# Seven block products for a convolution's input projections, and a modulation stream moved into the layer before it

## The chip, the cores and the metric

The kernel runs on one core of a Trainium2 chip, in one launch. The metric is the device time of one execution in microseconds, here the median of three runs. The times below come from these runs and from one execution recorded by the hardware profiler.

## The reference, cut to what matters

Two blocks follow each other. The change touches the second, which has two layers. Each layer has a mixer and a feed-forward part; shift, scale and gate of both come from a vector `c` (the modulation).

```python
for i in range(2):
    mods = silu(c) @ w_ada[i] + b_ada[i]          # 1024 -> 6 x 1024
    sh1, sc1, g1, sh2, sc2, g2 = split(mods, 6)
    h = rms_norm(x, norm1_g[i]) * (1 + sc1) + sh1
    mix = s5_mixer(h) if i == 0 else short_conv_mixer(h)
    x = x + g1 * mix
    h = rms_norm(x, norm2_g[i]) * (1 + sc2) + sh2
    x = x + g2 * swiglu(h)                        # hidden width 2816
return rms_norm(x, final_g)

def short_conv_mixer(h):
    bg, cg, v = split(h @ w_in, 3)                # 1024 -> 3 x 1024
    return (bg * causal_conv3(cg * v)) @ w_out
```

There are 1024 tokens of width 1024, all in float32.

## The kernel before, in words

Activations lie transposed: 128 channels on the partitions, tokens along the free axis, in two halves of 512. A float32 product is made of three matmuls in a reduced-width form: each operand is split into a high part (ScalarE, line 105) and a low part (VectorE, line 113), and `mm3` (lines 119 to 121) adds high x high, high x low and low x high. A weight block is 128 x 512 (four 128 x 128 tiles).

Feed-forward layers (`phase_ffn`) go through groups of hidden blocks: first the input products of the group's blocks, then the output products with all of the group, which are added to x in memory by accumulating transfers from the POOL queue (line 2058), or, in the last group, to x on the chip. The input products of one hidden block, two row blocks (gate and up) by 1024 tokens by 1024 channels, are a `Unit`: a 2 x 2 by 2 x 2 block product in seven half-size products instead of eight, each of 12 matmuls. Its weight sums (S1 to S4) are made on VectorE from four loaded blocks, its token sums (T1 to T4) once per layer by `Quad.make`. The results are put together on VectorE (line 1940). `ffn_head` runs the first three hidden blocks while the norm of the second token half still comes in: the first block by eight ordinary products, the next two by seven each, in an order that uses the early tokens first.

`Weights` is the feed-forward layers' stream: a list of entries (load, make). `take` hands out the next split block after `fill` has issued loads until six entries are under way (`near` and `ready` together) and made splits until four are ready. Raw blocks have six buffers, split pairs six, sums two. The loads are issued by SyncE in order. A stream is set up at a layer's start and ends with it.

The convolution (`phase_conv`) does not use it. `Normed` writes the normed tokens in two parts. For each of eight blocks and each token half, three ordinary gemms of 24 matmuls give cg, v and bg (tiles pc, pv, pb); VectorE and ScalarE form cg * v, the three taps and the product with bg. Loads and splits come from `e.wload`, emitted when the phase starts. Then x is copied on the chip, and the output products (tile pco) follow.

The modulation is computed by `ada` as a background generator: columns of `w_ada` are loaded (SyncE, line 1316), multiplied by silu(c) and added up on VectorE (lines 1322 and 1324), summed over the partitions by a matmul with ones (tile pada), copied by ScalarE and stored as a row in memory by SyncE (line 1338). `e.tick()` advances it. The first layer's feed-forward half and two of the second layer's six parts run in the mixer's output stage, in tiles of 1024 columns; the other four run in the convolution, in tiles of 512 columns with two buffers.

The order of instructions on each engine comes from the order of the calls and a scheduler that puts ready work of other engines in between; an engine runs its own instructions in that order.

Of the kernel before, what the change touches and what calls it, by code (L numbers as in the profile page):

```python
# [14 lines left out]
P = 128  # L15
# [21 lines left out]
class Env:  # L37


    def __init__(self, ctx, tc, d, out):  # L40
# [15 lines left out]
        self.ident_r = c.tile([P, P], F32R, name="ident_r")  # L56
# [190 lines left out]
def phase_projections(e):  # L247
# [152 lines left out]
    bif = np_.tile([36, 1], F32, name="bif")  # L400
# [385 lines left out]
def phase_attention(e, r1, x, done):  # L786
# [41 lines left out]
    nlam = np_.tile([P, 1], F32, name="nlam")  # L828
# [468 lines left out]
def ada(e, tiles, L, mods, step, wait, ahead, s0=0, s1=6, w=T):  # L1297
# [3 lines left out]
    if s0 == 0:  # L1301
        cact = e.const.tile([P, 8], F32, name=f"ada{L}c")
        e.tc.keep_in_program_order(nc.scalar.activation(cact, e.col("c"), AF.Silu))
        mods[L] = e.const.tile([P, 48], F32, name=f"ada{L}"), cact
# [34 lines left out]
    rr = e.t2("adrr")[0:n, 0:P]  # L1339
    nc.sync.dma_start(out=rr, in_=row)  # L1340
    bb = e.t2("adb")[0:n, 0:P]
    nc.sync.dma_start(out=bb, in_=d["b_ada"][L][8 * s0:8 * s1])
# [309 lines left out]
def phase_mixer(e, mods, x, n, fg, nxt):  # L1652
# [61 lines left out]
    e.bg += [ada(e, wada, 0, mods, 4, 2, 4, 3), ada(e, wada, 1, mods, 4, 2, 4, 0, 2)]  # L1714
# [106 lines left out]
class Weights:  # L1821
# [15 lines left out]
    def block(self, src, more=False):  # L1837
# [3 lines left out]
        def load():  # L1841
# [7 lines left out]
            self.more.tile([P, 4, P], F32R, tag=t, name=t, bufs=4) for t in ("wh", "wl")])  # L1849
# [40 lines left out]
    def fill(self, ahead):  # L1890
# [3 lines left out]
        while self.near and len(self.ready) <= ahead:  # L1894
            self.ready.append(self.near.pop(0)[1]())
# [59 lines left out]
class Normed(Next):  # L1955


    def __init__(self, e, mod, i, x, name):
        super().__init__(e, name, self.pairs)
        self.x = x  # L1960
        self.mod, self.i = mod, i
        self.hT = [{} for _ in range(NB)]

    def pairs(self, h, r):
        nc, i = self.e.nc, self.i
        R = self.e.spread(r, self.e.np_, self.name)
        for b in range(NB):
            if b and b % 2 == 0:
                yield
            t = self.e.t2("hx")  # L1970
            A = self.mod[:, 8 + 24 * i + b:9 + 24 * i + b]
            B = self.mod[:, 24 * i + b:24 * i + b + 1]
            nc.vector.scalar_tensor_tensor(out=t, in0=self.x[b][h], scalar=A, in1=R,
                                           op0=ALU.mult, op1=ALU.mult)
            hi, lo = self.hT[b][h] = pair(self.e, b, h, self.name)
            nc.scalar.activation(hi, t, AF.Identity, bias=B)
            nc.vector.scalar_tensor_tensor(out=lo, in0=t, scalar=B, in1=hi.bitcast(F32),
                                           op0=ALU.add, op1=ALU.subtract)


def phase_ffn(e, L, mod, inp, nxt, xp, last):

    nc, d, q = e.nc, e.d, inp.q
    W = Weights(e, 6, 6, 2, 3, 6)
    e.ap = e.tc.alloc_tile_pool(name="ap", bufs=1, reuse_waits="tile")
    src = lambda f: [d["w_ffn_in"][L, f + NF * i] for i in range(2)]
    a = {}

    def use(f):

        s = {}

        def take(n, t):
            h = int(n[1])
            s[h, int(n[0])] = t
            if n[0] == "0":
                nc.scalar.activation(t, t, AF.Silu)
            if (h, 0) in s and (h, 1) in s:
                nc.vector.tensor_tensor(out=s[h, 1], in0=s[h, 1], in1=s[h, 0], op=ALU.mult)
                if f not in a:  # L2000
                    a[f] = tuple(xp.tile([P, T], F32R, tag="x", name=f"a{p}", bufs=NB) for p in range(2))
# [3 lines left out]
    def plan():  # L2005
        for f0, f1 in FGROUPS:
            for f in range(max(f0, 3), f1):
                W.add(*W.unit(src(f), [Unit.left[p] for p in Unit.order]))
            if f1 - f0 == 4:
                W.add(*(W.block(d["w_ffn_out"][L, m, :, f0:f1], f1 == NF and m >= 4) for m in range(NB)))  # L2010
            else:
                W.add(*(W.block(d["w_ffn_out"][L, m:m + 2, :, f0:f1].rearrange("m p f c -> p m f c"))
                        for m in range(0, NB, 2)))

    for gi, (f0, f1) in enumerate(FGROUPS):
        end = gi == len(FGROUPS) - 1
        fs = list(range(f0, f1))
        if gi == 0:
            ffn_head(e, W, inp, src, use, plan)
            fs = fs[3:]  # L2020
        for f in fs:
            e.tick()
            Unit(e, W, q, use(f)).run(Unit.order)
        parts = nxt.parts if end else Next.parts
        if end:
            pool = last()
            W.more = e.tc.alloc_tile_pool(name="wt", bufs=1, side="right", reuse_waits="tile")
            for m in range(NB):
                t = pool.tile([P, T], F32, tag="x", name=f"x{m}", bufs=NB)
                e.x[m] = [t[:, half(h)] for h in range(2)]  # L2030
            for h in range(2):
                for m in range(NB):
                    nc.scalar.dma_start(out=e.x[m][h], in_=inp.xd[m][:, half(h)])
        wo = {}
        for m, i in (order(NB, NB - 1, len(parts)) if end else
                     [(m, h) for m in (0, 1) for h in (1,)] + [(m, 0) for m in (0, 1)]
# [374 lines left out]
```

## Time and profile before

| what | us |
|---|---|
| median of three runs (2900.1 to 2903.42) | 2900.79 |
| the profiled execution | 2904.91 |
| its span, first to last instruction | 2903.1 |
| first feed-forward layer, from its first product | 1182.5 to 1854.4 |
| convolution, input products | 1854.45 to 2128.8 |
| convolution, output products | 2128.8 to 2218.1 |
| second feed-forward layer, from its first product | 2220.6 on |

PE is TensorE, DVE is VectorE, ACT is ScalarE, SP is SyncE. Busy time of PE is modelled at the matmuls' ends, which overlap, so the spacing of two starts says more than a duration. A wait is given as the engine's idle time and what ended it.

### The profile page before, as it was taken

The numbers are of one execution on the slowest core, as the hardware profiler recorded it, in microseconds if no ns is written. First come the engines' busy times: TensorE is split into PE (matmuls) and PEld (weight loads), VectorE is DVE, ScalarE is ACT, GpSimd is POOL, SyncE is SP. The second block draws the span as 40 slices with busy tenths as digits, with TensorE's granted clock in tenths as the row PEclk, the third lists the DMA queues.
The fourth block names the chain that finished last, engine by engine and source line by source line (L and its number), as shares of the span: only waits on it lengthen the run. The fifth ranks groups of instructions, "written<-read, shape, count | busy, mean of one in ns | idle before, by whom it ended". The sixth has DMA issues, their size and how long they took to land.

```text
span 2903.1 us, 38535 instructions
## 1 busy us (share of the span) xinstructions
PE 2849.6 (98%) x14112; PEld 2327.7 (80%) x14112; DVE 1825.2 (63%) x3585; ACT 1218.3 (42%) x2251; POOL 207.1 (7%) x270
## 2 busy tenths in 40 slices
PE   8999999999999999999999999999999999999998
PEld 7888788877778777788888888788887888888887
DVE  7988556388967964866455446765246754645465
ACT  6244553366746621633333343422234433333343
POOL 0000000000001000010101120000010011010110
PEclk9999999999999999999999999999999999999999
DMA  6465227553234653152534553354132345253543
GB/s 220 158 224 185 93 75 245 178 177 110 84 95 169 224 178 126 49 103 72 105 82 86 101 103 92 108 171 139 47 131 70 78 86 100 70 103 86 96 94 124
DMA packets 174709, 351.00 MB, mean 121 GB/s; under 512 B 19124, under 2 KB 38900, under 8 KB 173496
## 3 DMA queue, kind: packets, MB, share of 16 engines
q1 hardware_dynamic: 139448, 281.42, 30.0%
q0 software_dynamic: 26880, 54.54, 11.7%
q10 hardware_dynamic: 8192, 12.59, 1.3%
q8 instruction: 111, 1.82, 0.3%
q14 instruction: 78, 0.64, 0.1%
HBM read 246.71 MB, written 97.57 MB: 119 GB/s over the span
## 4 chain that ended last, share of the span: by engine, by line
PE 75%; issue 6%; DVE 5%; ACT 1%; DMA 1%; POOL 0%; ACTq 0%; DVEq 0%; POOLq 0%; SPq 0%
PE pu L119 9%; PE pu L121 9%; PE pu L120 9%; PE po L120 5%; PE po L119 5%; PE po L121 5%; PE pout L119 1%; PE pout L120 1%; PE pout L121 1%; PE pS L871 1%; PE pc L121 1%; PE pc L119 1%; PE pc L120 1%; PE pco L119 1%; PE pco L120 1%
## 5 line engine op out<-in xcount | busy, mean ns | idle before, releaser
L113 DVE TENSOR_TENSOR wl<-raw,wh 128x512 fp32r<-128x512 f32 x292 | 199.8, 686 | 245.3 <-ACT wh L105 239.5
L105 ACT ACTIVATE wh<-raw 128x512 fp32r<-128x512 f32 x292 | 182.5, 629 | 345.9 <-PE pu L120 191.3
L121 PE MATMUL po<-a,wl 128*128 128x512 f32 (+1 forms) x736 | 279.5, 380 | 1.2 <-DVE wl L113 1.2
L119 PE MATMUL po<-a,wh 128*128 128x512 f32 (+1 forms) x736 | 279.7, 381 | 0.2 <-ACT wh L105 0.2
L120 PE MATMUL po<-a,wh 128*128 128x512 f32 (+1 forms) x736 | 279.7, 380 | 0.0
L120 PE MATMUL pu<-f,wh 128*128 128x512 f32 x672 | 261.4, 389 | 0.0
L121 PE MATMUL pu<-f,wl 128*128 128x512 f32 x672 | 261.4, 389 | 0.0
L119 PE MATMUL pu<-f,wh 128*128 128x512 f32 x672 | 261.4, 389 | 0.0
L105 ACT ACTIVATE wh<-wraw 128x512 fp32r<-128x512 f32 (+1 forms) x189 | 136.5, 727 | 231.9 <-PE pj L120 43.7
L113 DVE TENSOR_TENSOR wl<-wraw,wh 128x512 fp32r<-128x512 f32 (+1 forms) x189 | 151.9, 809 | 124.1 <-ACT wh L105 123.6
L2057 ACT ACTIVATE ev<-po,ada 128x512 f32<-128x512 f32 x160 | 109.0, 682 | 132.2 <-issue 56.8
L121 PEld LDWEIGHTS po<-a,wl 128*128 128x128 f32 x736 | 138.3, 188 | 28.0 <-DVE wl L113 2.1
L120 PEld LDWEIGHTS po<-a,wh 128*128 128x128 f32 x736 | 138.3, 188 | 27.1 <-DVE a L113 0.9
L119 PEld LDWEIGHTS po<-a,wh 128*128 128x128 f32 x736 | 138.2, 188 | 27.3 <-ACT wh L105 1.1
L121 PEld LDWEIGHTS pu<-f,wl 128*128 128x128 f32 x672 | 126.2, 188 | 26.3
L120 PEld LDWEIGHTS pu<-f,wh 128*128 128x128 f32 x672 | 126.2, 188 | 26.2
L119 PEld LDWEIGHTS pu<-f,wh 128*128 128x128 f32 x672 | 126.2, 188 | 26.0
L119 PE MATMUL pj<-h,wh 128*128 128x512 f32 x352 | 140.3, 398 | 0.0
L120 PE MATMUL pj<-h,wh 128*128 128x512 f32 x352 | 139.5, 396 | 0.0
L121 PE MATMUL pj<-h,wl 128*128 128x512 f32 x352 | 139.2, 396 | 0.0
L113 DVE TENSOR_TENSOR wl<-sum,wh 128x512 fp32r<-128x512 f32 x80 | 54.9, 686 | 80.5 <-ACT wh L105 80.5
L2058 POOL DMA_DIRECT2D f0x<-ev x80 | 68.2, 852 | 481.6 <-ACT ev L2057 479.0
(635 smaller groups left out, 7012.8 us busy)
## 6 DMA issues: line engine op xcount, KB each, us to landing
raw<-in_w_ffn_in SPq DMA_DIRECT2D x172, 256.0 KB
wada<-in_w_ada SPq DMA_DIRECT2D x64, 512.0 KB
raw<-in_w_ffn_out SPq DMA_DIRECT2D x88, 256.0 KB
f0x<-ev POOLq DMA_DIRECT2D x80, 256.0 KB, 4.4
f1x<-ev POOLq DMA_DIRECT2D x80, 256.0 KB, 4.4
wada<-in_w_ada SPq DMA_DIRECT2D x64, 256.0 KB
wraw<-in_w_in SPq DMA_DIRECT2D x28, 512.0 KB
wraw<-in_w_out SPq DMA_DIRECT2D x48, 256.0 KB
```

What stands on the lines that cost most here:

```text
L105: i = self.nc.scalar.activation(*a, **k)
L113: nc.vector.tensor_tensor(out=lo, in0=src, in1=hi.bitcast(F32), op=ALU.subtract)
L119: nc.tensor.matmul(out, lh, rh, start=first, stop=False)
L120: nc.tensor.matmul(out, lh, rl, start=False, stop=False)
L121: nc.tensor.matmul(out, ll, rh, start=False, stop=last)
L871: nc.tensor.matmul(o[m], self.q[a][ms, qs], self.k[c][b][ms, 0:wc], start=(i == 0), stop=(i == 2 and not lastp))
L2057: nc.scalar.activation(t, pt, AF.Copy, scale=g)
L2058: nc.gpsimd.dma_start(out=inp.xd[m][:, tok], in_=t, accum_op=ALU.add)
```

## The change

The convolution's input products become units of the same seven-product form. `ConvQuad` makes the token sums; its tiles for T1 and T2 lie in the pool that held the hidden activations. Two kinds of unit alternate: "cv" units pair the cg and v rows of one block, "b" units pair the bg rows of two blocks. The first three units run in the same head as a feed-forward layer's, now a class `Head` for all three. One `Weights` stream serves both feed-forward layers and the convolution; `load` puts the first three blocks of the convolution's head into it before the output products of the layer's last group, and the whole head of the second feed-forward layer before the convolution's output products.

All six parts of the second layer's modulation go into the stream of the first feed-forward layer (`ada_stream`): 12 columns of 512, each of eight tiles (load and one VectorE operation), an empty entry and a sum; they are spread evenly between the weight blocks, up to 16 blocks before the end. The loads use the stream's raw buffers. The mixer's output stage keeps the first layer's part. x is stored to memory during the first feed-forward layer's end and loaded again before the convolution's output products.

The identity matrix in reduced form gets a pool of its own that ends after the attention, and two one-column tiles are given a width of 32.

```diff
--- before.py
+++ after.py
-        self.ident_r = c.tile([P, P], F32R, name="ident_r")
...
+def ada_stream(e, W, L, mods):
+    nc, d = e.nc, e.d
+    m, cact = mods[L]
+    row = e.dr.tile([48, P], F32, name=f"ada{L}row")
+    st, steps = {}, []
+    none = lambda: None
+    def tile(o, k):
+        t = {}
+        def load():
+            t["raw"] = W.tile("raw").rearrange("p a b -> p (a b)")
+            nc.sync.dma_start(out=t["raw"], in_=d["w_ada"][L, k * P:(k + 1) * P, o * HT:(o + 1) * HT])
+        def make():
+            if k == 0:
+                st["acc"] = e.ap.tile([P, HT], F32, tag="adacc", name="adacc", bufs=1)
+                nc.vector.tensor_scalar(out=st["acc"], in0=t["raw"], scalar1=cact[:, 0:1], scalar2=None,
+                                        op0=ALU.mult)
+            else:
+                nc.vector.scalar_tensor_tensor(out=st["acc"], in0=t["raw"], scalar=cact[:, k:k + 1],
+                                               in1=st["acc"], op0=ALU.mult, op1=ALU.add)
+        return load, make
+    def sums(o):
+        def make():
+            pt = e.mm("aux", "pada")
+            nc.tensor.matmul(pt[0:64], e.ones[:, 0:64], st["acc"], start=True, stop=True)
+            rs = e.t2("adrow")[0:1]
+            nc.scalar.activation(rs, pt[0:1], AF.Copy)
+            nc.sync.dma_start(out=row[4 * o:4 * o + 4], in_=rs)
+        return none, make
+    def rows():
+        st["rows"] = ada_rows(e, L, row, 0, 6)
+    for o in range(12):
+        steps += [tile(o, k) for k in range(8)] + [(none, none), sums(o)]
+    return steps + [(none, rows)] + [(none, none)] * 3 + [
+        (none, lambda: ada_columns(e, L, m, 0, 6, *st["rows"]))]
...
-    e.bg += [ada(e, wada, 0, mods, 4, 2, 4, 3), ada(e, wada, 1, mods, 4, 2, 4, 0, 2)]
+    e.bg.append(ada(e, wada, 0, mods, 2, 2, 4, 3))
...
         while self.near and len(self.ready) <= ahead:
-            self.ready.append(self.near.pop(0)[1]())
+            w = self.near.pop(0)[1]()
+            if w:
+                self.ready.append(w)
...
+class ConvQuad(Quad):
+    def __init__(self, e, mod, i, x, name, xp):
+        super().__init__(e, mod, i, x, name)
+        self.xp, self.xt = xp, {}
+    def open(self):
+        self.pool = self.e.tc.alloc_tile_pool(name="cq", bufs=1, side="right", reuse_waits="tile")
+    def pair(self, c, k):
+        return tuple(self.tile(c, k, p, F32R) for p in range(2)) if c == "T1" else super().pair(c, k)
+    def tile(self, c, k, p, dt=F32):
+        if c == "T3":
+            return self.e.hp.tile([P, HT], dt, tag=f"h{k}1{p}", name=c + self.name, bufs=1)
+        if c == "T4":
+            return super().tile(c, k, p, dt)
+        if (c, k) not in self.xt:
+            self.xt[c, k] = self.xp.tile([P, T], dt, tag="x", name=c + self.name, bufs=NB)
+        return self.xt[c, k][:, half(p)]
...
+    def load(self, n=None):
+        n = len(self.todo) if n is None else n
+        self.W.add(*self.todo[:n])
+        del self.todo[:n]
...
+        n, k = len(todo) - 16, 0
+        for i, item in enumerate(todo):
+            W.add(item)
+            while k < len(extra) and k * n < (i + 1) * len(extra):
+                W.add(extra[k])
+                k += 1
...
+                then()
...
+class Conv:
+    def __init__(self, e, W, mod, xp, inp, nxt):
+        self.e, self.W, self.mod, self.xp, self.inp, self.nxt = e, W, mod, xp, inp, nxt
+        self.units = [u for b in range(0, NB, 2) for u in (("cv", b), ("cv", b + 1), ("b", b))]
+        self.yt, self.y, self.pend, self.yd = {}, {}, {}, set()
+        self.cw = e.col("conv_w2").rearrange("p (a b) -> p a b", b=3)
+        self.head = Head(e, W, inp, self.src, self.use)
+    def src(self, i):
+        kind, b = self.units[i]
+        w = self.e.d["conv_w_in"]
+        return [w[b + 8], w[b + 16]] if kind == "cv" else [w[b], w[b + 1]]
+    def use(self, i):
+        kind, b = self.units[i]
+        return self.values(b) if kind == "cv" else self.gates(b)
+    def gates(self, b):
+        def take(n, t):
+            self.pend[b + int(n[0]), int(n[1])] = t
+            self.gate()
+        return take
+    def gate(self):
+        for k in [k for k in self.pend if k in self.yd]:
+            y = self.y[k]
+            self.e.nc.vector.tensor_tensor(out=y, in0=y, in1=self.pend.pop(k), op=ALU.mult)
+    def values(self, b):
+        e, nc, s, cv = self.e, self.e.nc, {}, {}
+        stt = lambda o, a, sc: nc.vector.scalar_tensor_tensor(out=o, in0=a, scalar=sc, in1=o, op0=ALU.mult,
+                                                              op1=ALU.add)
+        def take(n, t):
+            h = int(n[1])
+            s[h, int(n[0])] = t
+            if (h, 0) not in s or (h, 1) not in s:
+                return
+            cv[h] = s[h, 1]
+            nc.vector.tensor_tensor(out=cv[h], in0=cv[h], in1=s[h, 0], op=ALU.mult)
+            if b not in self.yt:
+                self.yt[b] = self.xq.tile([P, T], F32, tag="x", name="yb", bufs=NB)
+            y = self.y[b, h] = self.yt[b][:, half(h)]
+            nc.scalar.activation(y, cv[h], AF.Copy, scale=self.cw[:, b, 2:3])
+            for k in (1, 2):
+                stt(y[:, k:HT], cv[h][:, 0:HT - k], self.cw[:, b, 2 - k:3 - k])
+            if len(cv) == 2:
+                for k in (1, 2):
+                    stt(self.y[b, 1][:, 0:k], cv[0][:, HT - k:HT], self.cw[:, b, 2 - k:3 - k])
+                self.yd |= {(b, 0), (b, 1)}
+                self.gate()
+        return take
+    def run(self, xq, then):
+        e, W, d, x, inp, nxt = self.e, self.W, self.e.d, self.e.x, self.inp, self.nxt
+        nc = e.nc
+        self.xq = xq
+        e.ap = e.tc.alloc_tile_pool(name="ap", bufs=1, reuse_waits="tile")
+        inp.open()
+        self.head.load()
+        for i in range(3, len(self.units)):
+            W.add(*W.unit(self.src(i), [Unit.left[p] for p in Unit.order]))
+        out = [(m, k) for m in range(NB) for k in range(2)]
+        W.add(*(W.block(d["conv_w_out"][m][:, 4 * k:4 * k + 4], 2 * (i >= 14)) for i, (m, k) in enumerate(out)))
+        self.head.run()
+        for i in range(3, len(self.units)):
+            Unit(e, W, inp.q, self.use(i)).run(Unit.order)
...
+                nc.gpsimd.dma_start(out=x[m][h], in_=inp.xd[m][:, half(h)])
...
+        W.more = e.tc.alloc_tile_pool(name="wt", bufs=1, reuse_waits="tile")
+        then()
...
-    phase_ffn(e, 0, mods[0][0], f0, c, e.xp, room(f0))
+    c = ConvQuad(e, mods[1][0], 0, x, "c", e.xp)
     f1 = Quad(e, mods[1][0], 1, x, "f1")
-    phase_conv(e, mods[1][0], mods, e.xp, pools[0], c, f1)
     fin = Final(e, fg2)
-    phase_ffn(e, 1, mods[1][0], f1, fin, e.xp, room(f1))
+    ffn0 = Ffn(e, W, 0, mods[0][0], f0, c, e.xp, room(f0))
+    conv = Conv(e, W, mods[1][0], e.xp, c, f1)
+    ffn1 = Ffn(e, W, 1, mods[1][0], f1, fin, e.xp, room(f1))
+    ffn0.run(ada_stream(e, W, 1, mods), lambda: conv.head.load(3))
+    conv.run(pools[0], ffn1.head.load)
+    ffn1.run([], lambda: None)
```

`Ffn` and `Head` are `phase_ffn` and `ffn_head` of before as classes, with the same steps.

## Rows read from the trace of the kernel before

**Rows 1.** The page: engine, busy us (share) and instructions; granted clock by slice.

```profile
PE 2849.6 (98%) x14112; PEld 2327.7 (80%) x14112; DVE 1825.2 (63%) x3585; ACT 1218.3 (42%) x2251; POOL 207.1 (7%) x270
...
PEclk9999999999999999999999999999999999999999
```

**Rows 2.** Busy time by stretch, columns in the first line; feed-forward, convolution input, output.

```profile
core 0: us, PE busy (x) PEld busy (x) DVE busy (x) ACT busy (x) POOL busy (x), PEclk, DMA share, GB/s
1854.45:2128.80 274.35, 270.84 (x1188) 219.81 (x1187) 147.48 (x243) 76.91 (x128) 2.71 (x4) 0.99 0.37 115
2129.00:2218.40 89.40, 89.40 (x403) 73.99 (x401) 41.04 (x68) 26.28 (x43) 15.88 (x29) 1.00 0.35 124
1262.00:1838.10 576.10, 575.39 (x2544) 475.53 (x2543) 298.75 (x467) 213.14 (x349) 69.23 (x81) 1.00 0.47 97
...
1316.00:1373.00 57.00, 57.00 (x253) 47.23 (x252) 40.32 (x63) 21.67 (x36) 0.00 (x0) 1.00 0.19 57
...
1393.00:1433.00 40.00, 40.00 (x179) 33.11 (x178) 8.32 (x12) 14.36 (x23) 12.76 (x15) 1.00 0.81 125
```

**Rows 3.** TensorE in order of time: steady products, start, us, engine, line.

```profile
1840.17 0.39 PE L119 MATMUL po<-a,wh 128*128 128x512 f32 x1
...
1854.22 0.39 PE L121 MATMUL po<-a,wl 128*128 128x512 f32 x1
```

**Rows 4.** Instructions on tile pc, duration min/median/max, first and last start.

```profile
L119 PE MATMUL pc<-c,wh x128: 389/389/628, 1854.5 to 2117.4; 128*128 128x512 f32 x128
```

**Rows 5.** TensorE in order of time at the convolution's start, and its stretch.

```profile
1855.59 0.39 PE L120 MATMUL pb<-c,wh 128*128 128x512 f32 x1
1859.01 0.50 PE L121 MATMUL pb<-c,wl 128*128 128x512 f32 x1 [3.04 <-DVE wl L113]
1859.35 0.39 PE L119 MATMUL pb<-c,wh 128*128 128x512 f32 x1
1860.21 0.50 PE L121 MATMUL pc<-c,wl 128*128 128x512 f32 x1 [0.47 <-DVE wl L113]
...
1863.66 0.63 PE L121 MATMUL pc<-c,wl 128*128 128x512 f32 x1
...
1864.43 0.39 PE L120 MATMUL pc<-c,wh 128*128 128x512 f32 x1
...
1854.00:1882.00 28.00, 24.49 (x108) 19.67 (x106) 22.97 (x42) 8.29 (x14) 1.01 (x1) 0.94 0.44 141
```

**Rows 6.** The same at the second and first feed-forward layer's start.

```profile
2218.14 0.39 PE L121 MATMUL pco<-cy,wl 128*128 128x512 f32 x1
2220.55 0.50 PE L119 MATMUL pha<-f,T3f 128*128 128x512 f32 x1 [2.02 <-ACT T3f L105]
...
2228.72 0.50 PE L207 MATMUL f1R<-f1dh,ones_r 128*128 128x512 f32 x1 [0.31 <-DVE f1dh L201]
...
1182.47 0.80 PE L119 MATMUL pha<-f,T3f 128*128 128x512 f32 x1 [3.23 <-ACT T3f L105]
...
1179.00:1194.00 15.00, 11.41 (x44) 8.78 (x43) 8.73 (x20) 7.39 (x14) 1.97 (x2) 0.77 0.27 87
...
2219.00:2260.00 41.00, 39.12 (x177) 31.79 (x178) 36.75 (x66) 26.36 (x46) 1.90 (x2) 1.00 0.14 46
```

**Rows 7.** VectorE by group in the convolution: count, busy us, mean ns, idle before.

```profile
L1324 DVE SCALAR_TENSOR_TENSOR adacc<-wada,ada1c,adacc 128x512 f32<-128x512 f32 x56 | 42.0, 750 | 30.1 <-DMA wada<-in_w_ada 29.9
...
L2139 DVE SCALAR_TENSOR_TENSOR yb<-cv,cols,yb 128x511 f32<-128x511 f32 x16 | 12.0, 749 | 4.5 <-ACT yb L2161 4.5
```

**Rows 8.** Waits of TensorE and of SyncE's queue: us in total, times, longest.

```profile
PE pada L1333 <- DVE adacc L1324: 1.7, 1, 1.7
...
SPq L1338 <- ACT adrow L1335: 68.3, 9, 16.0
```

More of the change, by code (lines that the diff above doesn't have):

```diff
@@ L1835, in add, with block @@
         self.todo += items
-    def block(self, src, more=False):
+    def block(self, src, more=0):
         st = {}
@@ L1952 @@
     done = {"2": ("00", "c"), "6": ("01", "q"), "7": ("11", "v"), "4": ("10", "u")}
[L1955 to L1978, printed above, removed]
@@ L1993, in take, with __init__, src, use @@
+class Ffn:
+    def __init__(self, e, W, L, mod, inp, nxt, xp, last):
+        self.e, self.W, self.L, self.mod, self.inp, self.nxt, self.xp, self.last = e, W, L, mod, inp, nxt, xp, last
+        self.a = {}
+        self.head = Head(e, W, inp, self.src, self.use)
+    def src(self, f):
+        return [self.e.d["w_ffn_in"][self.L, f + NF * i] for i in range(2)]
+    def use(self, f):
+        e, a, s = self.e, self.a, {}
         def take(n, t):
@@ L2002, in take, with plan @@
                 e.split(a[f][0][:, half(h)], a[f][1][:, half(h)], s[h, 1])
         return take
-    def plan():
+    def plan(self, extra):
+        W, w_out = self.W, self.e.d["w_ffn_out"]
+        todo = []
         for f0, f1 in FGROUPS:
             for f in range(max(f0, 3), f1):
-                W.add(*W.unit(src(f), [Unit.left[p] for p in Unit.order]))
+                todo += W.unit(self.src(f), [Unit.left[p] for p in Unit.order])
             if f1 - f0 == 4:
-                W.add(*(W.block(d["w_ffn_out"][L, m, :, f0:f1], f1 == NF and m >= 4) for m in range(NB)))
+                todo += [W.block(w_out[self.L, m, :, f0:f1], 4 * (f1 == NF and m >= 4)) for m in range(NB)]
@@ L2011, in plan @@
             else:
[L2012 to L2030, printed above, removed]
-            for h in range(2):
[L2032 to L2036, printed above, removed]
-                     + [(m, h) for m in range(2, NB) for h in range(2)]):
-            tok = parts[i]
-            if m not in wo:
-                w = W.take()
-                if f1 - f0 == 4:
-                    wo[m] = w
-                else:
-                    wo[m], wo[m + 1] = ([t[:, 2 * i:2 * i + 2] for t in w] for i in range(2))
-            pt = e.mm("mm", "po")[:, 0:tok.stop - tok.start]
-            w = wo[m]
-            for k in range(f1 - f0):
-                e.mm3(pt, (w[0][:, k], w[1][:, k]), (a[f0 + k][0][:, tok], a[f0 + k][1][:, tok]),
-                      k == 0, k == f1 - f0 - 1)
-            g = mod[:, 40 + m:41 + m]
-            if end:
-                x = e.xs(m, tok)
-                nc.vector.scalar_tensor_tensor(out=x, in0=pt, scalar=g, in1=x, op0=ALU.mult, op1=ALU.add)
-                nxt.done(m, i)
-            else:
-                t = e.ap.tile([P, HT], F32, tag="ev", name="ev", bufs=3)
-                nc.scalar.activation(t, pt, AF.Copy, scale=g)
-                nc.gpsimd.dma_start(out=inp.xd[m][:, tok], in_=t, accum_op=ALU.add)
```

302 lines of the change are left out of this document (162 added, 140 removed).

## The prediction

> **What bounds the kernel now.** I read the page first, for busy shares and the clock; then busy time in stretches, stage by stage; then TensorE's instructions in order of time at the ends of the stages; then VectorE by group and the list of waits. The page says TensorE: matmuls 98% of the span, VectorE 63%, granted clock near full all along [rows 1]. Since matmul ends are modelled, I take the spacing of starts instead. The 62 starts from 1840.17 to 1854.22 us lie (1854.22 - 1840.17) / 62 = 0.2266 us apart [rows 3], and this is the price of one 128x512 matmul here.
>
> In the convolution's input stage, from 1854.45 to 2128.80, there are 9 groups of 128 matmuls (three products, three passes each) [rows 4]: 1152 x 0.2266 = 261.0 us of 274.35 [rows 2]. The rest is a stop at its start and small matmuls. After 1882 TensorE waits for nobody there. In the feed-forward stage it is busy 575.39 of 576.10 us [rows 2]. So a matmul less is time less, as long as VectorE and the transfers keep up; the question is what the change asks of them.
>
> **The change part by part.**
>
> *Products.* Twelve units take the place of the 24 gemms. The first is computed in the ordinary way (8 products of 12 matmuls, 96), the other eleven by seven products of 12 (84): 96 + 924 = 1020 against 1152. Gone are 132 x 0.2266 = 29.9 us, all on the path.
>
> *Start of the convolution.* Before, its weights are loaded and split only when the feed-forward layer is over. TensorE stops from 1855.59 to 1859.01 for a low weight part, again before 1860.21, and eleven starts up to 1864.43 then take 4.22 us instead of 2.49 [rows 5]. That loses 3.19 + 0.63 + 1.73 = 5.5 us. After, the first three weight blocks (three products, 8 us of matmuls) are split during the last output products. What is late next is the token norm's spread; at the next layer's start, which has the same order of work, that costs 0.31 us plus a few tenths around it [rows 6]. I put 1.0 there, so 4.5 us go.
>
> *Start of the second feed-forward layer.* The wait of 2.02 us for a split weight block (2.41 between two starts, less 0.23) [rows 6] is removed, since the whole head is queued before the convolution's output products, which have 89.4 us with VectorE busy 41.04 [rows 2]. 2.2 us go.
>
> These two stops show a thing about the clock. The 3.04 us wait is followed by slow matmuls and a mean granted clock of 0.94, the 3.23 us one ahead of the first feed-forward layer by 0.77, the 2.02 us one by 1.00 [rows 5, 6]. The Trainium skill (TensorE: Matmul & The Clock Gate, HAM oscillation) has it that a TensorE left idle between bursts long enough drops to half clock and that each repeat pays again. By that rule each new wait in the first feed-forward layer would cost its own length and 1.7 us more, and the loss of 20 us in the second rival below would be 41 us, so slower than before. The rows speak against it for waits as short as that rival's.
>
> *Modulation of the second layer.* The closing matmuls stay the same in number and merely move (four 512-column sums from the mixer, eight from the convolution): nothing. In the mixer and the convolution the tiles go, where they stopped nobody for more than 1.7 us [rows 8]: I count nothing. They reappear in the first feed-forward layer: 96 loads of 256 KB, 96 VectorE operations, 12 sums with a row store each, spread as 125 entries over 161 weight blocks.
>
> Is there room? Three units there take 57.0 us, and VectorE is busy 40.32 of them [rows 2], 13.4 of 19.05 us per unit (84 x 0.2268). A unit has 7 blocks, hence 7 x 96 / 161 = 4.17 modulation operations. One takes 0.750 us, and in the old place waited 30.1 / 56 = 0.54 us on its transfer [rows 7], there with only two buffers. So 13.4 + 4.17 x 0.75 = 16.6 without waits and 18.8 with the old ones, against 19.05. It fits, without much room. In the output products VectorE is busy far less.
>
> Queues. SyncE's issues now hold modulation loads between weight loads, six raw buffers for both, and the order now issues a load with none or one block made before its use, where there were two. Each of the 12 row stores waits on SyncE for ScalarE's copy of the sum, and the loads behind it wait too. In the old places 9 such waits came to 68.3 us, at most 16.0 [rows 8]. VectorE's next work waits for those loads, and TensorE for VectorE, but up to four finished blocks stand ahead of TensorE (4 x 12 x 0.2266 = 10.9 us). A sum is also an instruction in TensorE's own queue: all products behind it wait if its accumulator is late. It is emitted two entries after the accumulator's last operation, at two to three blocks' distance (5.4 us or more), and the single accumulator makes VectorE's next column wait for it. Bounds: nothing if all of that is hidden, and 12 x 3.04 = 36 us if each closing stops TensorE as long as the longest wait for VectorE in rows 5. Of the old sums one waited, 1.7 us [rows 8]. The nearest row is that one; I take 3 us in all, that is two such waits.
>
> The same 16 transfer engines carry the accumulating stores of the output products: share 0.81 there [rows 2]. About five modulation tiles per output group come on top. In the unit stretch twelve 256 KB loads fill 0.19 of 57 us, 0.9 us each, so five add 4.5 us to 40, share 0.92. Below 1, nothing lost, but no reserve either; if stores then lag, ScalarE waits for an eviction buffer, which falls under the second rival.
>
> *Convolution stage, VectorE.* A values unit has 18 operations for products and weights as in the other layer, two products and four full-length taps (0.749 each [rows 7]): 20 x 0.61 + 4 x 0.75 = 15.2 us of 19.05, where 0.61 is 13.44 / 22. A gates unit has 22, 13.4 us. The modulation is gone from here, so it fits. Each tap pair waits for ScalarE's first tap. I take 2 us over the stage; the ends are nothing and, if a values unit took 21 us on VectorE, 8 x 2 = 16.
>
> *Rest.* 16 stores of x to memory and 16 reloads, on POOL's queue, replace copies there; the tiles that the reload fills come free two to three products (5 to 8 us) before the output products begin, and the first is wanted 5.4 us after: nothing. Tile padding and the identity's own pool: nothing. The splits before the output products wait for the last unit's last result, and 21 matmuls (4.8 us) of the first output product do not need it: nothing.
>
> Sum: -29.9 - 4.5 - 2.2 + 3 + 2 = -31.6 us. The profiled execution took 2904.91 (span 2903.1); it lies 4.1 above the median of 2900.79, and as the sum is a difference I take it from the median: 2900.8 - 31.6 = 2869 us.
>
> **The rivals.**
>
> *The forecast's own range*: charges of nothing to twice mine give 2864 to 2874; with 3 us for what the starts keep or lose it is 2861 to 2877.
>
> *The sums stop TensorE.* Each of the 12 costs 1.7 us as the one before did, 20 in place of 3: 2886, and with the convolution's 16 as well up to 2900. For it: a sum stands in TensorE's queue, and the loads behind a row store start late. Against: one wait in 12 before.
>
> *The weight stream of the first feed-forward layer falls behind (the slower side).* VectorE stands still for each modulation tile because its load comes too late in the shared buffers. The gain to be eaten is 36.6 less the convolution's 2, over 19 units 1.8 us each, so the point of turning is (19.05 + 1.8 - 13.44) / 4.17 - 0.75 = 1.03 us of wait per tile, about twice the 0.54 measured. At 1.5 us VectorE needs 13.44 + 4.17 x 2.25 = 22.8 us per unit, 3.8 x 19 = 72 us lost: 2938. For it: fewer blocks between load and use, and the row stores. Against: six buffers instead of two, weight loads half as dense as the other layer can take.
>
> *The convolution becomes VectorE's*: 16 us in place of 2, 2883.
>
> *The change does not do what it says*, that is the seven-product form saves matmuls but the head and sums give all back: about 2901. The matmul count speaks against it.
>
> **How the numbers follow.** Less than 0.2% (5.8 us) cannot be told from no change. Forecast 0.63; sums 0.18; convolution 0.07; falling behind 0.09; no change 0.03. Faster: 0.63 + 0.18 + 0.07 = 0.88; same 0.03; slower 0.09. The range takes the forecast's lower end with 4 us for a stop that vanishes wholly, 2860, and most of the sums' rival, 2892. Left out are the 0.12 of the last two cases and part of the sums.
>
> **What would show it.** 1020 matmuls of 128x512 in the convolution's input products, spaced 0.227; no wait above 1 us at the two starts; in the first feed-forward layer, stretches equal to the second's but for the sums; the wait of VectorE per modulation tile under 1.03 us. It is wrong if that layer's unit stretches show TensorE waiting for split weights or for the accumulator by more than 10 us in all, or if the convolution's units take over 20 us each.

## The result and the profile after

The changed kernel takes 2924.24 us (2921.38 to 2928.03, 4 runs), the kernel before, beside it, 2902.11 us (2900.10 to 2904.94, 4 runs). The ratio is 1.0076 with a 95% interval of 1.0059 to 1.0094: 22 us slower, where 32 us faster was forecast. The profiled execution of the changed kernel has a span of 2920.8 us.

The page of the changed kernel: engine, busy us (share of the span), instructions; then the granted clock by slice.

```profile
PE 2869.9 (98%) x13979; PEld 2296.9 (79%) x13979; DVE 1935.2 (66%) x3786; ACT 1243.8 (43%) x2295; POOL 216.4 (7%) x286
...
PEclk9999999999998999999999999999999999999999
```

Beside [rows 1], TensorE has 133 matmul records fewer and is busy 20 us longer. Its clock is no lower (0.991 over the whole span, 0.988 before). So each matmul has become longer, and not through a lower clock. Busy time by stretch says in which stages, columns as in [rows 2]. The four stretches are the first feed-forward layer, the convolution's input products, its output products and the second feed-forward layer, each from its first product to that of the next; the last one ends where the closing group of small matmuls begins. First the changed kernel, then the one before.

```profile
1180.93:1888.65 707.72, 702.72 (x2977) 552.53 (x2978) 452.98 (x727) 279.07 (x462) 78.44 (x96) 1.00 0.53 128
1888.65:2129.20 240.55, 240.01 (x1039) 193.22 (x1038) 205.48 (x348) 92.48 (x154) 11.11 (x19) 1.00 0.21 67
2129.20:2221.28 92.08, 92.08 (x403) 74.02 (x402) 53.13 (x88) 31.75 (x53) 9.22 (x16) 1.00 0.32 107
2221.28:2913.16 691.88, 690.20 (x3090) 560.06 (x3089) 381.70 (x617) 266.94 (x451) 71.69 (x84) 1.00 0.41 87
```

```profile
1182.47:1854.45 671.98, 670.29 (x2952) 553.22 (x2953) 387.85 (x618) 267.00 (x440) 70.66 (x82) 1.00 0.42 89
1854.45:2129.00 274.55, 271.04 (x1189) 219.97 (x1187) 147.68 (x243) 77.11 (x128) 2.92 (x5) 0.99 0.37 115
2129.00:2220.55 91.55, 89.53 (x403) 73.99 (x402) 41.81 (x70) 27.48 (x46) 16.42 (x30) 1.00 0.34 121
2220.55:2895.82 675.27, 673.61 (x3089) 561.06 (x3090) 388.91 (x631) 269.19 (x457) 71.29 (x83) 1.00 0.42 91
```

The convolution's input gains 34.0, as hoped. But the second feed-forward layer, whose products the change leaves as they were (3089 and 3090 matmul records), loses 16.6 us. The convolution's output products, 403 in both, lose 0.5 although a wait of 2.0 us at their end is gone, and the first feed-forward layer loses 35.7. A loss in a stage with the same products and hardly any idle time (690.20 of 691.88 us busy) must be each product's own price. TensorE in order of time in the second feed-forward layer (start, us, engine, line; `mm3` is on lines 118 to 120 in the changed kernel), 62 products without a wait:

```profile
2270.16 0.39 PE L120 MATMUL pu<-T2f,wl 128*128 128x512 f32 x1
...
2284.63 0.39 PE L119 MATMUL pu<-T4f,wh 128*128 128x512 f32 x1
```

(2284.63 - 2270.16) / 62 = 0.2334 us from start to start, against 0.2266 in [rows 3]: 3% more for each product. The same kernel shows both prices side by side. At the end of the first feed-forward layer, in one run of output products with the same tile names:

```profile
1875.45 0.39 PE L120 MATMUL po<-a,wl 128*128 128x512 f32 x1
...
1877.32 0.39 PE L119 MATMUL po<-a,wh 128*128 128x512 f32 x1
1877.55 0.39 PE L120 MATMUL po<-a,wl 128*128 128x512 f32 x1
...
1885.93 0.39 PE L118 MATMUL po<-a,wh 128*128 128x512 f32 x1
```

Up to 1877.55 nine products take 2.10 us, 0.2333 each; from there 37 take 8.38, 0.2265 each. What changes at 1877.55 is only the buffers from which weights come: until then the stream's old ones, then those set up for the convolution. By the addresses that the program, as built, gives its tiles, the tokens (the operand that is streamed) all start at 32 modulo 64 bytes in each partition, the old weight blocks at 0 (modulo 64) and the new ones at 32. The product at 1877.55 still has an old block itself; only the weights loaded behind it are new, and it is already fast. Over the 12 places of this kind where nothing else holds TensorE the mean is 0.228 us; at the 11 where new weights are followed by old ones it is 0.235.

That led to the theory tested below. I call **distance** the start of a matmul's streamed tokens less the start of the weights loaded for the following matmul, modulo 256 bytes. Of the 128x512 products of float32 parts, the kernel before has 8244 of 10134 at distance 0; the changed one has 1159 of 10002, and 7458 at 32. The change moves them without meaning to: it takes a 512-byte identity and 32 bytes of silu(c) out of the constants, which lie in front of every weight buffer, so the weights from the mixer's output on lie 544 bytes lower, while the tokens lie at the other end of the memory and stay. Of the 544 bytes the 512 are two whole periods of 256 and change no distance; the 32 bytes do. Each layer had its own tile of silu(c) and both now share one, which the section on the change does not name.

The waits that the prediction reckoned with are small. From the list of waits of the changed kernel: us in total, times, longest.

```profile
...
PE pha L118 <- ACT T3f L104: 3.2, 1, 3.2
...
PE po L120 <- DVE wl L112: 1.8, 2, 1.0
...
PE po L119 <- DVE a L112: 1.3, 1, 1.3
PE pu L118 <- ACT wh L104: 1.3, 1, 1.3
```

No line says that TensorE waited for a sum's accumulator. The 3.2 us is the old wait of [rows 6] at the first layer's start. At the second one's start the first product follows the last of the convolution without any wait:

```profile
2221.05 0.39 PE L120 MATMUL pco<-cy,wl 128*128 128x512 f32 x1
2221.28 0.39 PE L118 MATMUL pha<-f,T3f 128*128 128x512 f32 x1
```

And VectorE's group for the moved modulation waited 44.0 us for 84 tiles, 0.52 us each, almost all of it hidden from TensorE, which in that layer, after its start, waited 2.1 us in all for split weights:

```profile
L1390 DVE SCALAR_TENSOR_TENSOR adacc<-raw,adac,adacc 128x512 f32<-128x512 f32 x84 | 62.9, 749 | 44.8 <-DMA raw<-in_w_ada 44.0
```

### The profile page after: what moved, and what is told of

Its sections match the earlier page's. It is cut to its first block, busy times and chain, and to the rows that moved or that the text cites. A ratio compares the mean times of both kernels' runs of the same rounds, so it can differ in the third digit from the quotient of the medians.

```text
span 2920.8 us, 38609 instructions
## 1 busy us (share of the span) xinstructions
PE 2869.9 (98%) x13979; PEld 2296.9 (79%) x13979; DVE 1935.2 (66%) x3786; ACT 1243.8 (43%) x2295; POOL 216.4 (7%) x286
## 5 line engine op out<-in xcount | busy, mean ns | idle before, releaser
L104 ACT ACTIVATE wh<-raw 128x512 fp32r<-128x512 f32 x360 | 225.8, 630 | 464.3 <-PE pu L119 265.6
L112 DVE TENSOR_TENSOR wl<-raw,wh 128x512 fp32r<-128x512 f32 x360 | 245.6, 684 | 214.4 <-ACT wh L104 214.2
L120 PE MATMUL po<-a,wl 128*128 128x512 f32 (+1 forms) x736 | 282.9, 385 | 1.8 <-DVE wl L112 1.8
L119 PE MATMUL po<-a,wh 128*128 128x512 f32 (+1 forms) x736 | 283.2, 386 | 1.3 <-DVE a L112 1.3
L118 PE MATMUL po<-a,wh 128*128 128x512 f32 (+1 forms) x736 | 283.2, 386 | 0.2 <-ACT ev L2215 0.2
L118 PE MATMUL pu<-f,wh 128*128 128x512 f32 x672 | 266.2, 396 | 0.0
L119 PE MATMUL pu<-f,wh 128*128 128x512 f32 x672 | 265.4, 395 | 0.0
L120 PE MATMUL pu<-f,wl 128*128 128x512 f32 x672 | 265.4, 395 | 0.0
L120 PEld LDWEIGHTS po<-a,wl 128*128 128x128 f32 x736 | 138.1, 188 | 32.7 <-DVE wl L112 2.7
L112 DVE TENSOR_TENSOR wl<-wraw,wh 128x512 fp32r<-128x512 f32 (+1 forms) x125 | 108.0, 869 | 73.9 <-ACT wh L104 73.4
L104 ACT ACTIVATE wh<-wraw 128x512 fp32r<-128x512 f32 (+1 forms) x125 | 96.1, 776 | 138.4 <-PE pj L119 46.1
L120 PEld LDWEIGHTS pu<-f,wl 128*128 128x128 f32 x672 | 126.0, 187 | 30.8
L120 PE MATMUL pj<-h,wl 128*128 128x512 f32 x352 | 139.5, 396 | 0.0
L104 ACT ACTIVATE wh<-sum 128x512 fp32r<-128x512 f32 x100 | 62.5, 631 | 167.0 <-PE pu L119 130.8
L112 DVE TENSOR_TENSOR wl<-sum,wh 128x512 fp32r<-128x512 f32 x100 | 68.2, 682 | 76.2 <-ACT wh L104 76.2
```

The source lines that it names most:

```text
L104: i = self.nc.scalar.activation(*a, **k)
L112: nc.vector.tensor_tensor(out=lo, in0=src, in1=hi.bitcast(F32), op=ALU.subtract)
L118: nc.tensor.matmul(out, lh, rh, start=first, stop=False)
L119: nc.tensor.matmul(out, lh, rl, start=False, stop=False)
L120: nc.tensor.matmul(out, ll, rh, start=False, stop=last)
```

## The experiments

**Moving the weights, and moving the tokens.** In the changed kernel 32 bytes more among the constants put every weight buffer 32 bytes higher (a_left32):

```
-        self.mhalf = c.tile([P, 8], F32, name="mhalf")
+        self.mhalf = c.tile([P, 16], F32, name="mhalf")[:, 0:8]
```

> The changed kernel with one constant tile 32 bytes wider, so that every pool on the left side, the split weights among them, lies 32 bytes further. Theory (distance): a 128x512 matmul goes at 0.227 us when the moving operand and the next weight block start at the same place within 64 bytes, and at 0.233 us when they lie 32 bytes apart; the change moved the weights by an odd multiple of 32 bytes, which made 6953 more of them unequal. Here 9942 of 10002 are equal: 8768 x 0.0066 = 58 us less than the changed kernel, about 2862 us. Rival (stream): the loss comes from the modulation in the first feed-forward layer's weight stream: unchanged, 2924 us. Rival (place): weight blocks at a multiple of 64 bytes are slow, wherever the moving operand lies: also about 2862 us.

Measured: 2872.98 us (2871.06 to 2874.31), ratio to before 0.9897 (0.9883 to 0.9912). So 51 us of the changed kernel's time go with 32 unused bytes. In the second feed-forward layer of this run, 62 starts:

```profile
2312.38 0.39 PE L118 MATMUL pu<-f,wh 128*128 128x512 f32 x1
...
2326.44 0.39 PE L120 MATMUL pu<-f,wl 128*128 128x512 f32 x1
```

14.06 / 62 = 0.2268 us. The time was 11 us above what I expected, in the main because the projections, which I had thought to become fast too, stayed at 0.233: they now had distance 128, which a rule modulo 64 calls 0. To leave the weights where they are and move the tokens instead, a 32-byte tile was put at the other end of the memory (a_right32):

```
+    edge = tc.alloc_tile_pool(name="edge", bufs=1, side="right")
+    tc.nc.vector.memset(edge.tile([P, 8], F32, name="edge"), 0.0)
...
+    edge.release()
```

> The changed kernel with a 32-byte tile at the right edge, so that the token operands on the right side move by 32 bytes and the weights stay where the change put them. Distance: 9977 of 10002 equal, about 2862 us, matmuls 0.227 us apart. Place: the weights have not moved, so 0.233 us apart and 2924 us. Stream: 2924 us.

Measured: 2874.83 us, ratio 0.9902 (0.9887 to 0.9916). The 62 starts from 2317.77 to 2331.82 us of this run are 0.2266 us apart. It is not the weights' place but their place against the tokens. Then the same 32 bytes in the kernel before, which pull its aligned pair apart (b_left32):

```
-        self.mhalf = c.tile([P, 8], F32, name="mhalf")
+        self.mhalf = c.tile([P, 16], F32, name="mhalf")[:, 0:8]
```

> The kernel before, nothing of the change, with the constant tile 32 bytes wider. Distance and place: the weights of mixer, feed-forward layers and convolution move off the tokens' place; 8263 unequal against 1875, of which the projections' 1344 gain: 6388 x 0.0066 = 42 us slower, about 2943 us, with the projections 9 us faster and the rest slower. Stream: unchanged, 2902 us.

Measured: 2951.19 us, ratio 1.0169 (1.0151 to 1.0187), without any part of the change in it. The same stretch of this run:

```profile
2292.91 0.39 PE L119 MATMUL pu<-f,wh 128*128 128x512 f32 x1
...
2307.36 0.40 PE L121 MATMUL pu<-T3f,wl 128*128 128x512 f32 x1
```

14.45 / 62 = 0.2331 us. It is 8 us more than I expected, since the projections, now at distance 192, stayed at 0.2333 us. The rival that the modulation's stream cost these 51 us falls here: this kernel has no such stream, and a_left32 has it in full.

**The modulus.** Three more shifts of the weights in the changed kernel, by the same line with 24, 48 and 64 columns (64, 160 and 224 bytes more: a_left64, a_left160, a_left224):

> Control: the changed kernel with the constant tile 64 bytes wider, so that everything on the left moves by 64 bytes and every distance within 64 bytes stays. Distance and place: 2924 us, matmuls 0.233 us apart. Stream: 2924 us. If any shift helped (a chance of the layout), it would be faster.

Measured: 2919.66 us, ratio 1.0060 (1.0045 to 1.0075), pace in the input products of the feed-forward layers 0.2333. A shift by 64 bytes brings next to nothing back.

> The changed kernel with the constant tile 160 bytes wider. The weights of feed-forward layers and convolution then start 128 bytes from the tokens' place counted within 256 bytes, and the projections' weights 0 bytes. Theory 64 (equal within 64 bytes is enough, as in the runs before): all equal, 0.227 us everywhere, 2862 to 2873 us. Theory 256 (only a distance of 0 within 256 bytes is quick, which would explain why the projections, at 128 since the first shift, stayed at 0.233): feed-forward layers and convolution at 0.233, the projections at 0.227, about 2912 us.

> The changed kernel with the constant tile 224 bytes wider: feed-forward layers and convolution at a distance of 64 within 256 bytes, projections at 192. Theory 64: 0.227 us everywhere, 2862 to 2873 us. Theory 256: 0.233 us everywhere but in the attention's output products, about 2920 us.

Measured, one run each: 2906.80 and 2885.74 us. The instructions on tiles pj (projections) and pu (feed-forward) in the run with 160 bytes, and then on tile pu in the one with 224 bytes, with their duration min/median/max in ns:

```profile
L119 PE MATMUL pj<-h,wh x352: 387/389/481, 59.8 to 493.0; 128*128 128x512 f32 x176
L119 PE MATMUL pu<-f,wh x672: 390/393/404, 1180.4 to 2840.1; 128*128 128x512 f32 x168
```

```profile
L119 PE MATMUL pu<-f,wh x672: 388/394/398, 1182.9 to 2819.3; 128*128 128x512 f32 x168
```

With 160 bytes the projections have distance 0 and are fast, while the feed-forward layers, at 128, stay slow. So the period is longer than 128 bytes, and 256 fits all these runs. A longer one does not show: in the trace of before, 311 products lie at 0 and 7624 at 256 modulo 512 bytes, and they take 0.2272 and 0.2268 us. But 64 is not as slow as the rest: the run with 224 bytes was 34 us faster than I expected. The mean spacing by distance, over all products of the traces that follow one another without a wait:

```
distance, bytes     0       32      64      96      128            160     192     224
us per product      0.2268  0.2333  0.2290  0.2334  0.2325-0.2328  0.2342  0.2334  0.2333
```

The attention output's products are an exception by their own price (0.2294 at distance 0, 0.2341 at 160).

**All stages aligned.** To a_left32 the projections' pool is shifted by 128 bytes, so that 9935 of 10002 products are at distance 0 (a_both); and the kernel before gets its projections aligned the same way, by a wider copy of the same tile that makes the pool 224 bytes larger (b_early). The edit to a_left32:

```
-    bif = np_.tile([36, 32], F32, name="bif")[:, 0:1]
+    bif = np_.tile([36, 64], F32, name="bif")[:, 0:1]
```

> The changed kernel with the constant tile 32 bytes wider and the projections' own pool 128 bytes larger, so that 9935 of the 128x512 matmuls lie at a distance of 0 within 256 bytes. Theory 256: against the first shift alone (2873 us) the projections' 1322 matmuls go from 0.233 to 0.227: 8 us, with some of the 816 narrower ones as much as 5 more: 2860 to 2865 us. Theory 64: they were equal already, 2873 us.

> The kernel before with the projections' pool 224 bytes larger, so that its projections lie at 0 as well; its feed-forward layers and convolution did already. Both theories: 1322 x 0.0066 = 9 us and up to 5 for the narrower ones, 2888 to 2893 us. It is the kernel before on equal terms: against the run with both shifts it should stand 28 us higher, the change's own worth by the sum (31.6) less what its attention output gains by placing.

Measured: 2867.43 us (2864.88 to 2869.41), ratio 0.9881 (0.9866 to 0.9896), and 2899.02 us (2893.74 to 2904.00, 10 runs), ratio 0.9988 (0.9979 to 0.9998). In the second one the projections did become fast, as the instructions on tile pj show in the trace of before and in this one:

```profile
L119 PE MATMUL pj<-h,wh x352: 392/396/505, 59.6 to 500.8; 128*128 128x512 f32 x176
```

```profile
L119 PE MATMUL pj<-h,wh x352: 389/389/503, 60.6 to 495.2; 128*128 128x512 f32 x176
```

Their pace went from 0.2333 to 0.2271, but 1322 x 0.0062 = 8.2 us became only 4.5 us at the end of the stretch that holds them, whose first product starts 1.0 us later in this trace, and 3 us of the whole. Where the rest went I did not trace. The two kernels of this pair differ by the change and, in the attention output alone, by distance (515 products at 160 in the one before, 0.2341 against 0.2294, 2.4 us). At equal distances the change is thus worth 2867.4 - 2899.0 + 2.4 = -29 us; from a_left32 and the kernel before, corrected in the same way (2.3 there and 1322 x 0.0006 = 0.8 in the projections), it is -26. The distances do not undo the change; they lie on top of it.

**Which weights.** From a_both, a spacer puts only the low weight blocks off by 32 bytes (wl32):

```
+                self.gap = self.pool.tile([P, 8], F32, tag="gap", name="gap", bufs=1)
...
+            tiles = hi, self.tile("wl", F32R)[:, 0:n]
```

> Edit: a_both with a spacer of 32 bytes a partition between the high and the low halves of the streamed weight blocks, so that the low halves alone lie 32 bytes off the moving operand (modulo 256), and the matmuls just before a low block, 2278 of the 128x512 ones (1483 of them in the feed-forward layers' first products), see a distance of 224 to the weights loaded next, the other 7667 of 0. Theory 'next weights' (TensorE's pace is set by where the moving operand lies against the weights loaded for the following matmul): the second matmul of each triple (high weights, low tokens) runs at 0.233 us, the first and the third at 0.227; about 2278 x 0.0065 = 15 us longer than a_both, near 2882 us. Rival 'own weights': the third matmul of each triple, whose own weights are the low block, is the slow one and the second is not; the total is the same, so the pace by place in the triple decides. Rival 'not the distance': all three stay at 0.227 and the time is a_both's 2867.

Measured, one run: 2914.11 us, 47 more than a_both and not 15. On tile pu, the three products of a triple:

```profile
L118 PE MATMUL pu<-f,wh x672: 387/395/506, 1182.1 to 2846.9; 128*128 128x512 f32 x168
...
L119 PE MATMUL pu<-f,wh x672: 392/400/401, 1182.3 to 2847.2; 128*128 128x512 f32 x168
...
L120 PE MATMUL pu<-f,wl x672: 389/389/397, 1182.5 to 2847.4; 128*128 128x512 f32 x168
```

By spacing they take 0.233, 0.239 and 0.228 us, 0.6998 for the three. The low block's own product (L120) is the fast one, and the slowest is the one ahead of it, during which the low block is loaded: the rival "own weights" falls, as does "not the distance". But the first product is slowed as well, though its own and the next weights are both aligned, so the distance as defined does not cover this mixed case. And the three together cost just what three cost when all are off (3 x 0.2333 = 0.6999). So a price per misaligned load, on which my 15 us rested, is wrong: one such load in three costs as much as three. Why is open; I did not try it with the high blocks off alone.

**The price of the moved stream.** From a_both the stream is left out (no_stream):

```
-    ffn0.run(ada_stream(e, W, 1, mods), lambda: conv.head.load(3))
+    tc.nc.vector.memset(mods[1][0], 0.0)
+    ffn0.run([], lambda: conv.head.load(3))
```

> Edit: a_both without the second layer's modulation stream; left out are its 96 loads, 96 VectorE passes, 12 sums, its biases and columns, so the second layer's scales and shifts are zero and everything computed from them differs. It prices the moved stream at equal pace of the matmuls. Theory 'the single sums cost what the double ones did': 12 sums of about 1.1 us and some 4 us of waits go, so the first feed-forward layer takes about 674 us instead of 691.9 and the whole about 2849 us. Rival, the prediction's own step (the stream adds 3 us, the sums nothing): about 2864 us. Rival 'the stream's loads hold up the weights': over 25 us fewer, under 2842 us.

The loads, VectorE operations and sums of the second layer's modulation are gone with it, and its scales and shifts are zero, so this run only prices them. Measured: 2846.99 us (2844.92 to 2847.96), 20.4 under a_both, as expected to 2 us. The first feed-forward layer in a_both and in this run:

```profile
1169.52:1861.43 691.91, 685.88 (x2978) 552.83 (x2978) 451.78 (x727) 278.20 (x462) 78.33 (x96) 1.00 0.54 131
```

```profile
1165.81:1838.98 673.17, 669.96 (x2953) 552.18 (x2953) 392.70 (x628) 271.85 (x449) 78.33 (x96) 1.00 0.42 97
```

18.7 us, of which the sums are most. TensorE around one sum in the changed kernel, and around a pair of them in the kernel of the next experiment:

```profile
1333.16 0.39 PE L120 MATMUL pu<-T4f,wl 128*128 128x512 f32 x1
1333.48 1.07 PE L1397 MATMUL pada<-adacc,ones 128*64 128x512 f32 x2
1334.49 0.50 PE L118 MATMUL pu<-f,wh 128*128 128x512 f32 x1
1334.83 0.40 PE L119 MATMUL pu<-f,wh 128*128 128x512 f32 x1
```

```profile
1397.23 0.39 PE L120 MATMUL po<-a,wl 128*128 128x512 f32 x1
1397.55 1.08 PE L1398 MATMUL pada<-adacc,ones 128*64 128x512 f32 x4
1398.56 0.50 PE L118 MATMUL po<-a,wh 128*128 128x512 f32 x1
1398.90 0.39 PE L119 MATMUL po<-a,wh 128*128 128x512 f32 x1
```

From the product ahead to the second one behind, 1.67 us pass in both, with two products' worth in it (0.467 and 0.453): 1.20 us for one sum, 1.22 for two side by side on 64 columns each (x4 against x2). Twelve single sums are 14.4 of the 18.7 us. Waits of TensorE make up 2.8 more: beside the 3.2 us at the layer's start, a_both has five of 0.2 to 1.4 us in this layer's products (4.2 in all), the run without the stream three of 0.2 to 0.7 (1.4). The last 1.5 us I do not assign.

**Sums in pairs.** The kernel before took its sums two at a time (12 pairs in all); the changed one keeps six pairs and turns the six others into twelve single sums. From a_both, paired again, with five raw buffers for room (pair5):

```
-            nc.tensor.matmul(pt[0:64], e.ones[:, 0:64], st["acc"], start=True, stop=True)
+            for j in range(2):
+                nc.tensor.matmul(pt[64 * j:64 * j + 64], e.ones[:, 0:64], st[o + j], start=True, stop=True)
...
-    W = Weights(e, 6, 6, 2, 3, 6)
+    W = Weights(e, 6, 5, 2, 3, 6)
```

> Edit: a_both with the modulation's sums taken two columns at a time, as the kernel before took them: two accumulators, the two sums side by side on 64 rows each, one copy of the full width, and two row writes; for room the stream has five raw buffers instead of six. Theory 'a pair of side-by-side sums costs what one alone costs': six of about 1.1 us go, about 6.6 us fewer than a_both, near 2861 us. Rival 'sums cost nothing or cost by the column': a_both's 2867 us. Rival 'one raw buffer fewer slows the stream, and TensorE then waits for weights or sums': above 2870 us.

Measured: 2858.81 us (2858.45 to 2859.27), ratio to before 0.9851 (0.9835 to 0.9868), 8.6 under a_both. Its first feed-forward layer:

```profile
1170.63:1852.27 681.64, 676.79 (x2978) 551.21 (x2979) 451.19 (x726) 275.34 (x456) 78.35 (x96) 1.00 0.53 133
```

10.3 us less than a_both, six sums' worth (7.2) and 3 us that I do not assign. One raw buffer fewer did no harm. This kernel, the change with 32 and 128 unused bytes and the sums in pairs, is the fastest of the complete ones, 44 us under the kernel before.

## Why the prediction was wrong

The step that failed is the first one: "0.2266 us apart [rows 3], and this is the price of one 128x512 matmul here". I took a price from one stretch and held it for all products on both sides of the change. It holds for one placement of the operands, and the change altered the placement. At 7458 products in the feed-forward layers, the convolution and the mixer's output it cost 0.0065 us more each, 48.5 us, and a_left32, which puts back just the 32 bytes, gives back 51 us (some 2 of them in the projections, which it moved from 160 to 128). None of the rivals had it. Only one line of the prediction touches on where tiles lie: "Tile padding and the identity's own pool: nothing." It gives no reason. The identity's 512 bytes did change nothing, but only as two whole periods of 256; the padding, together with the 32 bytes, moved the projections from 224 to 160 (0.2333 to 0.2342 us) and the attention output from 160 to 0 (0.2341 to 0.2294). The trace of before could have warned me: in it the projections have a median of 396 ns and a spacing of 0.2333 us without a wait, the feed-forward products 389 and 0.2267, for the same form and the same full clock. I read one stretch and did not ask why another stage paid 3% more. Of the signs that the prediction named, only the spacing of 0.227 could catch this; neither the waits nor the time of the convolution's units did.

Point by point, at equal distances (a_both):

- *Products.* Right: at equal distances the convolution's input stage is 234.4 us, 40.2 less than before: 29.9 for the 132 products, as computed, and 4 x 1.22 = 4.9 for the four pairs of sums that left it, which I had put at nothing.
- *Start of the convolution.* Right: the remaining 5.4 us, where I had 4.5 less 2 for VectorE. In the trace after, TensorE waits there once, 0.5 us, and its granted clock from 1886 to 1914 us is 1.00, against 0.94 at this place before. The 2 us for VectorE did not come.
- *Start of the second feed-forward layer.* Right: the 2.41 us between two starts became 0.23.
- *Modulation.* Mis-sized: "The closing matmuls stay the same in number ... nothing". They do, but two that ran side by side cost one, and the change took six pairs apart: 18 stops of 1.2 us instead of 12, 7.2 us. At equal pace the first feed-forward layer costs 19.9 us more than before: 14.4 for the sums, 2.8 for waits and 2.7 that I do not assign; the stages that lost the pairs give back 7.3. That I had 3 us for waits is luck: I had them for the accumulators of the sums, and they are waits for weights, activations and evictions.
- *Room on VectorE and the queue.* Right: the wait per tile is 0.52 us where 0.54 was taken and 1.03 was the point of turning. Row stores held the queue eight times for 35.9 us in all (at most 11.3) and TensorE felt little of it.
- *The clock.* The new waits in the first feed-forward layer are 1.3 us at most (1.4 in a_both), and its granted clock in the changed kernel is 1.00 from 1192 us to its end, so the clock added nothing to them.
- *The sums as a rival.* TensorE never waited for an accumulator; the sums cost their own time, not a wait.

The sum of -31.6 us is thus -26 to -29 measured. It came that near partly by luck, since the sums cost more than I had and the convolution gained more. The sign was turned by a term that stood nowhere in it, the pace of the products themselves.

The Trainium skill (SBUF — State Buffer, Who interferes with whom) says that TensorE has two independent read ports, one for the streamed operand and one for loading weights, and that it never waits on anyone. No run here tests what another engine's access does to TensorE. But two wholly independent reads would not make the pace depend on where the two operands start relative to each other, and with only that changed the pace went from 0.2268 to 0.2333 us and back. Here the measurement decides; that the two reads meet in the memory is argued from it, not shown.

## What to carry to other kernels

When TensorE is busy almost all the time, a stage that the change does not touch is the control: compare its spacing of starts before and after first. If that moved without waits and at the same clock, look at where the program places its tiles; here a few unused bytes in front of a pool were worth more than a new algorithm. And count a small matmul by the stops it makes in the stream of large ones, not by its columns.

## What the runs showed of the hardware

- The spacing of 128x512 products depends on the distance of the streamed operand from the next weights, modulo 256 bytes: 0.2268 us at 0, 0.2290 at 64, 0.2325 to 0.2342 at the other multiples of 32, at a granted clock of 1.00 (2.4 GHz). The attention output's products take 0.2294 at 0. The list of waits shows nothing of it, and the busy share stays at 98%.
- One misaligned load in three slows the triple as much as three do (0.6998 and 0.6999 us; one run, the low block alone off).
- Two 64-column sums side by side hold TensorE for 1.22 us, a single one for 1.20.
- What in the memory makes the difference is not shown. The addresses are known, but no trace has a row for it. The loads of the next weights take as long in both kernels (median 187 ns after, 188 before); it is the product whose record grows, from 389 to 396 ns. The second product of a triple, before, then after:

```profile
L120 PEld LDWEIGHTS pu<-f,wh x672: 187/188/188, 1194.0 to 2838.5; 128*128 128x128 f32 x168
L120 PE MATMUL pu<-f,wh x672: 389/389/398, 1194.2 to 2838.7; 128*128 128x512 f32 x168
```

```profile
L119 PEld LDWEIGHTS pu<-f,wh x672: 187/187/190, 1191.1 to 2855.7; 128*128 128x128 f32 x168
L119 PE MATMUL pu<-f,wh x672: 389/396/398, 1191.3 to 2855.9; 128*128 128x512 f32 x168
```
